# A trunk layer on one core: the mixer norm's strided sums replaced by a diagonal, and the softmax's division moved to GpSimd

## The chip, the cores and the metric

One core of a Trainium2 chip runs the whole layer. The metric is device microseconds (us) of one execution, the median of several runs. The engines are called by the names of the profile: PE (TensorE, with PEld for its weight loads), DVE (VectorE), ACT (ScalarE), POOL (GpSimd) and SP (the queue that issues the weight DMAs).

## The reference

The layer takes 512 tokens of 1024 features. It runs a half-step SwiGLU, then a mixer, a second half-step SwiGLU, a gated embedding and a last RMSNorm. The change lies in the mixer:

```
u = rmsnorm(h, g_mix)
z = u @ w_in                      # q, k, v (8 heads of 64), forget gate, SSM input
logits = q k^T / 8 + c_q - c_k    # c: running sum of log forget gates, causal mask
w = softmax(logits)               # rows in blocks of 128 queries
attn = w @ v
ssm  = s5_mixer(SSM input)        # runs beside the attention
h = h + concat(rmsnorm(attn), rmsnorm(ssm)) @ w_out
```

Everything is float32. Each matrix product is done as three products of split operands (a high part of type fp32r and the rest).

## The kernel before, in words

**Layout and order.** Activations lie with features on the partitions and the 512 tokens along the free axis, eight tiles `X[k]` of 128x512. The kernel's instructions are put out by hand in one order: `run` goes through a list of units; each has two steps, a step being some 12 matmuls on PE. Around each step, `run` takes one slot: it splits the weights of the next unit on ACT (`whi`) and DVE (`wlo`), runs evictions that have come due (`evicts`), advances the generators in `chains` by one `yield` before the step and by one after it, and runs what was put into `late` and `posts`. Each engine executes its own instructions strictly in that order. Weights come over SP's queue into five `wraw` tiles.

**The mixer's norm.** `Norm.chain` turns the accumulated squares `acc` (128 features x 512 tokens) into the reciprocal root mean square of each token. For each block of 128 tokens it multiplies `acc` as the stationary operand by a column of constants (line 316), which gives a sum for each token, tokens on the partitions. DVE adds EPS (line 322), POOL raises to the power -1/2 (line 323, `rc`), PE broadcasts `rc` over all partitions with four products by the identity (line 327), and ACT copies that to `r` (line 331, tile `rbc`). For the mixer's norm `n2` the chain is called with `strided=True`: four more sums are then taken over every fourth token, `acc[:, i::4]` (line 319), since the SSM input is computed with tokens j, j+4, j+8, ... on the partitions. Columns 4 to 7 of `rc` scale that input in `ssm_chain` (`ut`, line 714), columns 0 to 3 scale `v`. This chain runs while PE computes the forget gate's unit (lines 961 and 962, two steps of 8 matmuls).

**The attention.** It is a generator that advances with the slots from the second query/key unit on, beside the SSM's generator. Two heads (h2 = 0, 1) go together, in three stages: query blocks 0 and 1 (rows of 128 and 256 keys), block 2 (384) and block 3 (512). `SCORES` sets the slot n in which a stage's scores are multiplied (lines 1054, 1055, after the step). Then: at n+1, before the step, DVE adds the mask and takes the row's minimum (`exps`, line 1067; the sign is turned, so it is the maximum), and ACT gets the exponentials with their sums; at n+2, before the step, `divide` (lines 1080 and 1083): DVE takes the reciprocal of the sums and multiplies each block's row by it; at n+3, after the step, PE transposes the probabilities (`turn`, line 1091); at n+4 ACT and DVE split them (`pa`, `pb`, `pc`); `values_out` multiplies by `v` (lines 1136, 1137). PSUM is a ring of eight banks, `tmp` a ring of ten tiles of 128x512. POOL's own work in this stretch is the eight casts of `selr` into `qsel` (line 1034), two for each pair of heads, and the two DMA issues of `pr` (line 1226).

The two places in the code:

```
act(x, x, AF.Exp, scale=-1.0, bias=mn[h2][:, j:j + 1], accum_out=rs[h2][:, j:j + 1])
...
for hp, st in plan.get(n - 1, []):
    *state[hp, st], exp = exps(st, state[hp, st])
    late.insert(at_front, exp)
for hp, st in plan.get(n - 2, []):
    state[hp, st] = divide(st, *state[hp, st])
yield
...
chain_at(u_s[0], n2.chain(strided=True, wait=2))
```

Of the kernel before, what the change touches and what calls it, by code (L numbers as in the profile page):

```python
# [13 lines left out]
ADD, SUB, MUL = ALU.add, ALU.subtract, ALU.mult  # L14
# [28 lines left out]
def hybrid_trunk_kernel(ctx: ExitStack, tc: tile.TileContext, xT, pT, w13a, w2a, w13b, w2b, wqk, wv, ws, wf,  # L43
                        wglu, wout, wgate, wproj, cols, bf, ssm_s, ssm_bc, dskip, outT, dbg=None):
    nc = tc.nc
    V, S, G, T = nc.vector, nc.scalar, nc.gpsimd, nc.tensor
# [8 lines left out]
    def nm(base):  # L55
        n_name[0] += 1
        return f"{base}_{n_name[0]}"
# [7 lines left out]
    def tmp(shape=(128, 512), base="t"):  # L65
        return pool.tile(list(shape), F32, name=nm(base), tag="tmp", bufs=10)

    def small(shape, base="sm"):
        return pool.tile(shape, F32, name=nm(base), tag="small", bufs=12)

    def bank():
        return psum.tile([128, 512], F32, name=nm("ps"), tag="ps", bufs=8)
# [21 lines left out]
    ident = const.tile([128, 128], F32, name="ident")  # L94
# [160 lines left out]
    class Norm:  # L255
# [52 lines left out]
        def chain(self, strided=False, wait=0):  # L308
            for _ in range(2 * wait):
                yield  # L310
            yield
            one = ones[:, 0:1] if self.width == D else ones[:, 1:2]
            ps = bank()
            n = 8 if strided else 4
            for i in range(4):
                T.matmul(ps[:, i:i + 1], self.acc[:, i * 128:(i + 1) * 128], one, start=True, stop=True)  # L316
            if strided:
                for i in range(4):
                    T.matmul(ps[:, 4 + i:5 + i], self.acc[:, i::4], one, start=True, stop=True)
            yield  # L320
            ms, rc = small([128, 8], "ms"), small([128, 8], "rc")
            V.tensor_scalar(ms[:, 0:n], ps[:, 0:n], EPS, None, ADD)
            G.tensor_tensor(rc[:, 0:n], ms[:, 0:n], mhalf[:, 0:n], ALU.pow)
            yield
            ps = bank()
            for i in range(4):
                T.matmul(ps[:, i * 128:(i + 1) * 128], rc[:, i:i + 1].to_broadcast([128, 128]), ident,  # L327
                         start=True, stop=True)
            yield
            r = pool.tile([128, L], F32, name=nm("rbc"), tag="rbc", bufs=2)  # L330
            S.copy(r, ps)
            self.r, self.rc = r, rc
            yield


# [703 lines left out]
    def attention(qk, vs, nrm_a):  # L1039
# [38 lines left out]
        def divide(st, lg, rs):  # L1078
            for h2 in range(2):
                V.reciprocal(rs[h2][:, 0:len(BLOCKS[st])], rs[h2][:, 0:len(BLOCKS[st])])  # L1080
                for j, (i, c0) in enumerate(BLOCKS[st]):
                    x = lg[h2][:, c0:c0 + (i + 1) * 128]
                    V.tensor_scalar(x, x, rs[h2][:, j:j + 1], None, MUL)
            return lg

        def turn(st, lg):
# [75 lines left out]
        for n in range(VALUES[3] + 2):  # L1162

            at_front = len(late)
            for hp, st in plan.get(n - 4, []):
                if st == 0:
                    pt[hp] = probs()
                late.extend(split_probs(st, state.pop((hp, st)), pt[hp]))
            if po is not None:
                late.extend(gather(*po))  # L1170
                po = None
# [6 lines that stand above are left out]
            for hp, st in plan.get(n, []):  # L1178
                state[hp, st] = scores(hp, st)
            if n in VALUES:  # L1180
                hp = VALUES.index(n)
                po = hp, values_out(hp, pt.pop(hp))
            for hp, st in plan.get(n - 3, []):
                state[hp, st] = turn(st, state[hp, st])
            yield
# [391 lines left out]
```

## Time and profile before

| | |
|---|---|
| median of 3 runs | 1016.0 us (1014.75 to 1016.76) |
| profiled execution, its own time | 1014.84 us |
| its span | 1013.1 us |
| mean granted clock of TensorE | 0.995 |
| PE busy | 1000.1 us, 99% of the span |
| DVE busy | 663.0 us, 65% |
| ACT busy | 420.4 us, 41% |
| POOL busy | 44.6 us, 4% |

The profiled execution is 1.2 us faster than the median of the runs, and 1.7 us of its time lie outside the span. Busy time of PE counts a matmul to its modelled end; the spacing of two matmuls' starts tells more about its pace than their durations. The granted clock is a share of 2.4 GHz: 1.00 is 2.4 GHz and 0.50 is 1.2 GHz.

### The profile page before, as it was taken

The numbers are of one execution on the slowest core, as the hardware profiler recorded it, in microseconds if no ns is written. First come the engines' busy times: TensorE is split into PE (matmuls) and PEld (weight loads), VectorE is DVE, ScalarE is ACT, GpSimd is POOL, SyncE is SP. The second block draws the span as 40 slices with busy tenths as digits, with TensorE's granted clock in tenths as the row PEclk, the third lists the DMA queues.
The fourth block names the chain that finished last, engine by engine and source line by source line (L and its number), as shares of the span: only waits on it lengthen the run. The fifth ranks groups of instructions, "written<-read, shape, count | busy, mean of one in ns | idle before, by whom it ended". The sixth has DMA issues, their size and how long they took to land.

```text
span 1013.1 us, 13761 instructions
## 1 busy us (share of the span) xinstructions
PE 1000.1 (99%) x4988; PEld 840.8 (83%) x4988; DVE 663.0 (65%) x1321; ACT 420.4 (41%) x799; POOL 44.6 (4%) x52
## 2 busy tenths in 40 slices
PE   9999999999999999999999999999999999999996
PEld 7888888888878889888887888888888888888896
DVE  6678688767655564889998865444455446655465
ACT  6333233332343343468896443332332224434332
POOL 0430000001000001000101000000000000000000
PEclk9999999999999999999999999999999999999998
DMA  6423323233245332122112232333323335533002
GB/s 209 150 90 91 109 94 103 78 91 105 94 104 130 95 85 74 63 67 87 55 52 79 88 94 94 102 91 99 105 93 87 97 107 157 165 85 105 32 1 83
DMA packets 58244, 96.06 MB, mean 95 GB/s; under 512 B 10224, under 2 KB 17008, under 8 KB 58176
## 3 DMA queue, kind: packets, MB, share of 16 engines
q1 hardware_dynamic: 57920, 94.63, 30.9%
q8 instruction: 39, 0.64, 0.3%
q0 software_dynamic: 256, 0.56, 0.2%
q14 instruction: 29, 0.24, 0.1%
HBM read 91.89 MB, written 2.10 MB: 93 GB/s over the span
## 4 chain that ended last, share of the span: by engine, by line
PE 88%; DVE 7%; ACT 3%; issue 1%; DMA 0%; POOL 0%; SPq 0%; POOLq 0%; DVEq 0%; ACTq 0%
PE ps L236 28%; PE ps L238 28%; PE ps L237 28%; PE ps L1455 1%; DVE wlo L75 1%; DVE rot L75 1%; DVE lg L1067 1%; DVE qkhl L75 1%; ACT lg L81 1%; PE ps L327 1%; DVE rc L75 1%; PE ps L316 0%; PE ps L1091 0%; PE ps L640 0%; DVE U L738 0%
## 5 line engine op out<-in xcount | busy, mean ns | idle before, releaser
L236 PE MATMUL ps<-xhl,whi 128*128 128x512 f32 x816 | 320.3, 393 | 0.0
L238 PE MATMUL ps<-xhl,whi 128*128 128x512 f32 x816 | 317.8, 390 | 0.0
L237 PE MATMUL ps<-xhl,wlo 128*128 128x512 f32 x816 | 317.7, 389 | 0.0
L160 ACT CAST whi<-wraw 128x512 fp32r<-128x512 f32 x324 | 195.8, 607 | 240.2 <-PE ps L238 177.4
L75 DVE TENSOR_TENSOR wlo<-wraw,whi 128x512 fp32r<-128x512 f32 x324 | 215.5, 670 | 5.8 <-ACT whi L160 5.6
L238 PEld LDWEIGHTS ps<-xhl,whi 128*128 128x128 f32 x816 | 153.2, 188 | 32.4
L236 PEld LDWEIGHTS ps<-xhl,whi 128*128 128x128 f32 x816 | 153.2, 188 | 32.1 <-issue 1.0
L237 PEld LDWEIGHTS ps<-xhl,wlo 128*128 128x128 f32 x816 | 153.3, 188 | 31.1
L236 PE MATMUL ps<-h,whi 128*128 128x512 f32 x352 | 137.3, 390 | 0.0
L238 PE MATMUL ps<-h,whi 128*128 128x512 f32 x352 | 137.0, 389 | 0.0
L237 PE MATMUL ps<-h,wlo 128*128 128x512 f32 x352 | 137.0, 389 | 0.0
L78 DVE SCALAR_TENSOR_TENSOR x<-ps,x 128x512 f32<-128x512 f32 x48 | 33.2, 691 | 95.2 <-PE ps L238 95.1
L78 DVE SCALAR_TENSOR_TENSOR t<-ps,rbc 128x512 f32<-128x512 f32 x44 | 30.3, 690 | 76.5 <-PE ps L238 76.5
L238 PEld LDWEIGHTS ps<-h,whi 128*128 128x128 f32 x352 | 66.1, 188 | 13.8
L237 PEld LDWEIGHTS ps<-h,wlo 128*128 128x128 f32 x352 | 66.1, 188 | 13.7
L236 PEld LDWEIGHTS ps<-h,whi 128*128 128x128 f32 x352 | 66.1, 188 | 13.6
L75 DVE TENSOR_TENSOR t<-ps,rbc 128x512 f32<-128x512 f32 x44 | 30.4, 691 | 71.1 <-PE ps L238 65.0
L81 ACT ACTIVATE th<-t 128x512 f32<-128x512 f32 x44 | 27.8, 632 | 91.1 <-DVE t L75 91.1
L362 ACT CAST h<-t 128x512 fp32r<-128x512 f32 x44 | 27.4, 622 | 80.2 <-DVE t L75 80.2
L81 ACT ACTIVATE xhl<-x,colt 128x512 fp32r<-128x512 f32 x32 | 23.0, 725 | 47.8 <-DVE x L78 41.1
L236 PE MATMUL ps<-xhl,gw 128*128 128x256 f32 x128 | 36.5, 285 | 0.0
L238 PE MATMUL ps<-xhl,gw 128*128 128x256 f32 x128 | 36.2, 283 | 0.0
(256 smaller groups left out, 1134.5 us busy)
## 6 DMA issues: line engine op xcount, KB each, us to landing
wraw<-w13b SPq DMA_DIRECT2D x88, 256.0 KB, 2.9
wraw<-w13a SPq DMA_DIRECT2D x84, 256.0 KB, 2.8
wraw<-w2a SPq DMA_DIRECT2D x32, 256.0 KB, 2.7
wraw<-w2b SPq DMA_DIRECT2D x32, 256.0 KB, 2.7
wraw<-wqk SPq DMA_DIRECT2D x16, 256.0 KB, 2.8
wraw<-wout SPq DMA_DIRECT2D x16, 256.0 KB, 2.8
wraw<-wgate SPq DMA_DIRECT2D x16, 256.0 KB, 2.9
wraw<-w2a SPq DMA_DIRECT2D x16, 192.0 KB, 2.4
```

The costliest lines, as they stand in the source:

```text
L75: V.tensor_tensor(out, a, b, op)
L78: V.scalar_tensor_tensor(out, a, s, b, op0, op1)
L81: S.activation(out, in_, f, **kw)
L160: S.copy(hi[:, 0:n], w[:, 0:n])
L236: T.matmul(ps, lh, rh, start=start, stop=False)
L237: T.matmul(ps, ll, rh, start=False, stop=False)
L238: T.matmul(ps, lh, rl, start=False, stop=stop)
L327: T.matmul(ps[:, i * 128:(i + 1) * 128], rc[:, i:i + 1].to_broadcast([128, 128]), ident, start=True, stop=True)
L362: S.copy(hl[:, 0, :], box["t"])
L1067: V.tensor_tensor_reduce(lg[h2][:, c0:c0 + n], pss[h2][:, c0:c0 + n], maskp[:, 512 - n:512], 1.0, 3e38, ADD, ALU.min, mn[h2][:, j:j + 1])
L1455: T.matmul(box0[wi], fw[wi][2 if i == 1 else 1][:, k], n1.pair(k)[i == 2], start=k + i == 0, stop=k + i == KD + 1)
```

## The change

The norm's four strided sums go. In their place, after `r` (the broadcast reciprocal, the same in all partitions) is there, DVE takes from every fourth column of `r` the diagonal: it multiplies by the identity and sums along the row, so that partition p gets the value of token 4p + j. The multiplication of the probabilities goes from DVE to POOL; the reciprocal stays on DVE.

```
--- before.py
+++ after.py
@@ -311,12 +311,9 @@
             one = ones[:, 0:1] if self.width == D else ones[:, 1:2]
             ps = bank()
-            n = 8 if strided else 4
+            n = 4
             for i in range(4):
                 T.matmul(ps[:, i:i + 1], self.acc[:, i * 128:(i + 1) * 128], one, start=True, stop=True)
-            if strided:
-                for i in range(4):
-                    T.matmul(ps[:, 4 + i:5 + i], self.acc[:, i::4], one, start=True, stop=True)
             yield
@@ -330,6 +327,11 @@
             r = pool.tile([128, L], F32, name=nm("rbc"), tag="rbc", bufs=2)
             S.copy(r, ps)
             self.r, self.rc = r, rc
+            if strided:
+
+                dg = tmp((128, 4, 128), "dg")
+                for j in range(4):
+                    V.tensor_tensor_reduce(dg[:, j], r[:, j::4], ident, 1.0, 0.0, MUL, ADD, rc[:, 4 + j:5 + j])
             yield
@@ -1080,7 +1082,7 @@
                 for j, (i, c0) in enumerate(BLOCKS[st]):
                     x = lg[h2][:, c0:c0 + (i + 1) * 128]
-                    V.tensor_scalar(x, x, rs[h2][:, j:j + 1], None, MUL)
+                    G.tensor_scalar(x, x, rs[h2][:, j:j + 1], None, MUL)
             return lg
```

## Rows read from the trace of the kernel before

**Rows 1.** The page: busy time, share of the span and instructions of each engine.

```profile
PE 1000.1 (99%) x4988; PEld 840.8 (83%) x4988; DVE 663.0 (65%) x1321; ACT 420.4 (41%) x799; POOL 44.6 (4%) x52
```

**Rows 2.** Busy time by stretch: from:to, length, engines, PEclk, DMA share, GB/s.

```profile
386.00:387.00 1.00, 1.00 (x4) 0.52 (x3) 0.46 (x1) 0.00 (x0) 1.00 (x1) 0.50 0.02 4
...
546.40:548.00 1.60, 1.60 (x13) 1.46 (x12) 0.52 (x2) 0.22 (x1) 0.18 (x1) 1.00 0.47 145
```

**Rows 3.** Timeline around the mixer norm's sums: start, us, engine, instruction, [idle before].

```profile
380.39 0.39 PE L961 MATMUL ps<-xhl,wfh 128*64 128x512 f32 x1
...
382.23 0.95 PE L316 MATMUL ps<-ones,acc 128*128 128x1 f32 x8
...
383.04 2.00 PE L319 MATMUL ps<-ones,acc 128*128 128x1 f32 x8
...
384.90 0.42 PE L961 MATMUL ps<-xhl,wfh 128*64 128x512 f32 x1
...
385.33 2.04 POOL L323 TENSOR_TENSOR rc<-ms,mhalf 128x8 f32<-128x8 f32 x1 [80.19 <-DVE ms L322]
...
389.17 0.60 PE L236 MATMUL ps<-whi,xhl 128*128 128x512 f32 x1
```

**Rows 4.** Timeline of PE at the SSM output norm's broadcast.

```profile
550.17 1.05 PE L327 MATMUL ps<-ident,rc 128*128 128x128 f32 x8
550.98 0.48 PE L236 MATMUL ps<-xhl,whi 128*128 128x512 f32 x1
```

**Rows 5.** Timeline of ACT and DVE behind the mixer norm's chain.

```profile
389.45 0.59 ACT L331 COPY rbc<-ps 128x512 f32<-128x512 f32 x1 [10.98 <-PE ps L327]
...
391.19 0.68 DVE L75 TENSOR_TENSOR fz<-ps,fl 8x512 f32<-8x512 f32 x1 [4.73 <-ACT fl L968]
...
404.95 0.48 DVE L714 TENSOR_SCALAR ut<-ps,rc 128x256 f32<-128x256 f32 x1 [1.06 <-ACT ut L81]
```

**Rows 6.** Groups of DVE instructions from 460 to 545 us, by form: xcount | busy, mean ns.

```profile
L1067 DVE CUSTOM_DVE_ANT_0 lg<-ps,maskp 128x128 f32<-128x128 f32 x8 | 2.3, 282 | 0.0
```

**Rows 7.** Busy time from 460 to 545 us, all engines, then line 1083 alone.

```profile
460.00:545.00 85.00, 81.88 (x432) 69.16 (x431) 83.14 (x235) 75.74 (x195) 5.19 (x8) 1.00 0.20 63
...
460.00:545.00 85.00, 12.80 (x32) 1.00 0.20 63
```

**Rows 8.** Timeline of PE in the attention.

```profile
471.01 0.82 PE L1091 MATMUL ps<-ident,lg 128*128 128x128 f32 x6
...
474.44 0.22 PE L1054 MATMUL ps<-kcum,qsel 128*128 128x128 f32 x1
475.62 0.30 PE L1055 MATMUL ps<-qkhl,qkhl 128*128 128x128 f32 x1 [0.96 <-DVE qkhl L75]
...
534.14 0.88 PE L1091 MATMUL ps<-ident,lg 128*128 128x128 f32 x6 [1.52 <-ACT pp L81]
```

**Rows 9.** Who waited for whom, 460 to 545 us: us in total, times, longest.

```profile
ACT kcum L1015 <- DVE qk L78: 3.8, 3, 1.8
```

**Rows 10.** Groups of POOL instructions, whole span, by form: xcount | busy, mean ns.

```profile
L323 POOL TENSOR_TENSOR rc<-ms,mhalf 128x4 f32<-128x4 f32 x5 | 6.2, 1232 | 471.4 <-DVE ms L322 471.4
L1034 POOL CAST qsel<-selr 64x512 fp32r<-64x512 f32 x8 | 5.3, 662 | 111.4 <-PE ps L1054 111.0
...
L1353 POOL TENSOR_TENSOR o<-xg,r 128x256 f32<-128x256 f32 x2 | 1.4, 722 | 1.9 <-ACT r L1347 1.9
```

**Rows 11.** Timeline of POOL and DVE around the divisions.

```profile
467.84 1.42 POOL L1034 CAST qsel<-selr 64x512 fp32r<-64x512 f32 x2 [79.12 <-PE ps L1054]
...
468.07 0.72 DVE L1083 TENSOR_SCALAR lg<-lg,rs 128x128 f32<-128x128 f32 x2
468.72 0.15 DVE L1080 RECIPROCAL rs<-rs 128x2 f32<-128x2 f32 x1
...
485.16 0.82 DVE L1083 TENSOR_SCALAR lg<-lg,rs 128x128 f32<-128x128 f32 x2
...
523.24 0.55 DVE L1083 TENSOR_SCALAR lg<-lg,rs 128x128 f32<-128x128 f32 x2
```

More of the change, by code (lines that the diff above doesn't have):

```diff
@@ L313, in chain @@
             ps = bank()
-            n = 8 if strided else 4
+            n = 4
             for i in range(4):
                 T.matmul(ps[:, i:i + 1], self.acc[:, i * 128:(i + 1) * 128], one, start=True, stop=True)
-            if strided:
-                for i in range(4):
-                    T.matmul(ps[:, 4 + i:5 + i], self.acc[:, i::4], one, start=True, stop=True)
             yield
@@ L332, in chain @@
             self.r, self.rc = r, rc
+            if strided:
+                dg = tmp((128, 4, 128), "dg")
+                for j in range(4):
+                    V.tensor_tensor_reduce(dg[:, j], r[:, j::4], ident, 1.0, 0.0, MUL, ADD, rc[:, 4 + j:5 + j])
             yield
@@ L1082, in divide @@
                     x = lg[h2][:, c0:c0 + (i + 1) * 128]
-                    V.tensor_scalar(x, x, rs[h2][:, j:j + 1], None, MUL)
+                    G.tensor_scalar(x, x, rs[h2][:, j:j + 1], None, MUL)
             return lg
```

## The prediction

> **What bounds the kernel now.** I read the page first. PE is busy for 1000.1 of 1013.1 us [rows 1], so over the whole span only two things can save time: matmuls that go, or come faster, and places where PE waits. A change on DVE or POOL counts only through the second. Then I asked for the two stretches that the diff touches, as timelines and as busy time by stretch, since a share over the span says nothing of them.
>
> The first stretch is the mixer norm, 380 to 390 us. The reader is to see three things in rows 3 and 2. The four plain sums take from 382.23 to 383.04, 0.81 us, and the four strided sums from 383.04 to 384.90, 1.86 us: more than twice as long for the same count. After them PE's granted clock is 0.50, that is 1.2 GHz [rows 2]. So the forget gate's second step and the broadcast, which follow, run at half pace: from 384.90 to 389.17, 4.27 us [rows 3]. Last, POOL's power over eight columns lasts 2.04 us [rows 3], and PE needs it for the broadcast.
>
> The second stretch is the attention, 460 to 545 us. There DVE is the fullest engine: busy for 83.14 of 85.00 us, against 81.88 for PE and 75.74 for ACT; the divisions are 12.80 us of DVE's time in 32 instructions [rows 7]. PE waits here, which it hardly does elsewhere. I add up, from start to start, what each late instruction took beyond the same step at a place without a wait. There are six such places; the first is 474.44 to 475.62 us, where the score product waits for DVE's `qkhl`, and the last is the transposes that start at 534.14 us, 1.5 us idle behind ACT [rows 8]. Together they make 4.8 us; by the records alone PE is idle for 85.00 − 81.88 = 3.1 us [rows 7], but a wait also spreads two starts whose records touch. ACT, for its part, waits three times, 3.8 us in all, for DVE's `qk` [rows 9]: DVE's lateness is passed on to ACT, and ACT's to PE through the PSUM banks.
>
> **The change part by part.**
>
> *The strided sums go.* The forget gate's second step then starts at 383.04 instead of 384.90 us. Its eight matmuls took 382.23 − 380.39 = 1.84 us in the first step, at full clock [rows 3], so the broadcast is due at 384.88 us. Its input: the power began 385.33 − 384.90 = 0.43 us after the last sum had been followed by the next matmul [rows 3], so now at 383.47; over four columns it takes 1.23 us (mean of five) [rows 10] and ends at 384.70, just in time. The broadcast takes 550.98 − 550.17 = 0.81 us where the clock is full [rows 4], so the next unit's first matmul comes at 385.69 instead of 389.17 us: 3.5 us. This takes the clock to stay at 1.00. For it speaks that the same four sums without the strided ones, at the SSM output norm, are followed by 1.00 [rows 2], as at the kernel's other norms. Against it: only here do the sums lie between matmuls that load 64 columns instead of 128 [rows 3]. If the clock falls all the same, what is left is the removed time, 1.9 us. Ends: −1.9 and −3.5; I take −3.5, since the nearest rows are those of the other norms.
>
> *The diagonal.* Four reduces of 128x128 on DVE. The nearest row is the masked minimum of that size, 0.28 us [rows 6]; four are 1.1 us. Reading every fourth column may cost more; with twice the price it is 2.3 us. DVE has been idle for 4.73 us when its next instruction starts at 391.19 [rows 5]; the reduces can begin only when ACT has copied `r`, at 389.45 + 0.59 = 390.04 [rows 5], so the cheap price is hidden entirely and the dear one delays the forget gate's small chain by 1.1 us, whose result the attention wants some 70 us later. The first reader of the new columns, `ut`, comes at 404.95 [rows 5], 13 us on. If that cover were gone, the delay would hit the SSM's input by at most 2.3 us. The extra tile takes one of ten in `tmp`'s ring for about a microsecond. Cost: 0 (0 to 0.3).
>
> *The divisions on DVE go.* DVE is relieved of 12.80 us in 85 [rows 7]. What is late today because DVE is late: the score product at 475.62, three groups of transposes that wait for banks, and ACT's waits. ACT is next: 75.74 us of work in a stretch that would be 85.0 − 4.8 = 80.2 us long, 94%. So I expect the waits behind DVE to go and the last one, behind ACT at 534.14 us, to stay for the greater part: ACT loses its waits, but PE arrives earlier too. I keep 1.5 us of the 4.8.
>
> *The divisions on POOL.* The trace has no such instruction. They have one tensor input, 32 of them with 2 x 4 x (128 + 256 + 384 + 512) = 10,240 elements per partition. Nearest below: the cast, one input, 662 ns for 512 elements, 1.29 ns each; above: the two-input product, 722 ns for 256, 2.82 ns each [rows 10]. That is 13.2 to 28.9 us for all. I take 15, nearer to the cast, which also has one input. POOL does 5.19 us of other work in the 85 [rows 7], so it is not full in either case. Is it in time? The tightest place is the first stage: the second reciprocal (468.72 us, some 468.1 when no division stands ahead of it) to the transposes at 471.01 [rows 8, 11] leaves 2.9 us for 768 elements, that is 1.0 to 2.2 us of work. The other stages' transposes stand further behind. So no wait of PE: 0, and with all at the dear end and slowed, up to 1 us at the first stage. What stands behind the divisions in POOL's queue: the casts of `qsel` and the two DMA issues of `pr`. The casts at 467.84 would come after the first divisions and end at 471.8 us at the latest; they are read at 474.44 [rows 8, 11]. The DMA issues move back to the unit in which they are written, and still stand ahead of the projection units by several steps. SP's queue is untouched.
>
> *What POOL takes from DVE.* While POOL casts, two divisions on DVE took 0.72 and 0.82 us; with POOL idle, 0.55 [rows 11]. So DVE lost up to 0.27 of 0.82 us, 33%, where both read and write SBUF. On 15 us of POOL work, with half of DVE's instructions reading two SBUF tensors, I put the loss at 15 x 0.33 x 0.5 = 2.5 us of DVE's time (0 to 9.5 us, the latter from 28.9 x 0.33). DVE keeps a relief of about 10 us, enough for the above; I put another 0.3 us of PE's waits on it. The Trainium skill (SBUF — State Buffer, "Who interferes with whom") says more: a DVE instruction with two SBUF inputs and a GpSimd instruction that reads SBUF exclude each other for the whole instruction. The rows show a loss of a third under the casts, not a full stop; by the page's rule the relief would be eaten, which is the second rival.
>
> *Sum:* −3.5 + 0 − (4.8 − 1.5 − 0.3) = −6.5 us. On the profiled execution's own 1014.84 us this gives 1008.3; the median of the runs stands 1.2 us higher, so I forecast 1009.5 us.
>
> **The rivals.**
>
> *The clock falls anyway* (0.50 after the sums, between matmuls of 64 columns). Then −1.9 − 3.0: 1011.1 us. The other norms speak against it.
>
> *The relief is eaten.* Each microsecond of POOL is taken from DVE: 83.14 − 12.80 + 13.2 = 83.5 us, DVE is as full as before, PE's waits stay, and only the norm's 3.5 us are won: 1012.5 us. The 33% of rows 11 speaks against a full loss; that DVE's instructions with two SBUF inputs under a POOL that reads 128 partitions aren't in the trace speaks for it. With the first rival on top it is 1014.1 us, no change.
>
> *Slower: POOL blocks DVE at the dear price.* If POOL needs 28.9 us and all of that is DVE's loss, DVE has 83.14 − 12.80 + 28.9 = 99.2 us to do in 85, and PE follows: 1016.0 − 3.5 + 14.2 = 1026.7 us. It decides where DVE's loss is more than 12.80 + 3.5 = 16.3 us, that is over 56% of POOL's dear time. 33% lies below that.
>
> **How the numbers follow.** The forecast has 57%, the clock that falls 11%, the eaten relief 18%, both at once 6%, the slower case 8%. The likeliest case's own range is from −8.3 (3.5 and all 4.8 us) to −4.5: 1007.7 to 1011.5 us. The range of 8 in 10 takes in the first two rivals: 1007.4 to 1013.2 us. Measurement tells about 0.2%, 2 us, from no change: faster means below 1014.0, which holds for the forecast and for the first two rivals but for their upper ends: 83%. Within 0.2%: both at once and some of the eaten relief, 10%. Slower: 7%.
>
> **What the profile after would show.** Right: no line for strided sums, the granted clock at 1.00 throughout 382 to 390 us, and the distance from the plain sums to the next unit's first matmul 3.46 us instead of 6.94; four reduces on DVE just ahead of `fz`; DVE below 90% in the attention, POOL at about 20 us there; no wait for `qkhl`; a shorter wait or none of ACT for `qk`. Wrong: 0.50 behind the sums; two-input DVE instructions of 128x512 well above the 0.68 us of `fz` [rows 5] while POOL divides; transposes that wait for POOL's `lg`; or an ACT so full that PE's waits move behind it unshortened. The last is the weakest step: 1.5 us kept of 4.8 is a judgement between 0 and all.

## The result, and the profile after

The changed kernel takes 1009.4 us (median of 4 runs, 1009.11 to 1009.82) against 1015.6 us for the kernel before on the same chip (4 runs, 1014.75 to 1016.76): 0.9939 of its time, with a 95% interval of 0.9925 to 0.9953. On another chip it took 1010.1 against 1015.45 us, 0.9947 (0.9934 to 0.9961). The forecast was 1009.5 us.

The profiled execution took 1009.63 us, with a span of 1007.9 us. The page's busy times, beside [rows 1]:

```profile
PE 996.2 (99%) x4980; PEld 838.5 (83%) x4980; DVE 655.1 (65%) x1297; ACT 420.7 (42%) x799; POOL 83.8 (8%) x84
```

POOL has 39.2 us more to do, while DVE has lost only 7.9 us. That is the first surprise: the divisions were 12.80 us on DVE, and 13.2 to 28.9 us had been put down for POOL.

Next, busy time by stretch (from:to, length, PE, PEld, DVE, ACT, POOL, granted clock, DMA share, GB/s): the norm, the microsecond that was at 0.50 in [rows 2], and the attention from its first score product to the first matmul behind its last value product.

```profile
382.23:386.00 3.77, 3.77 (x24) 2.70 (x23) 0.77 (x2) 0.00 (x0) 2.01 (x2) 1.00 0.15 22
386.00:387.00 1.00, 1.00 (x8) 1.00 (x8) 0.00 (x0) 0.41 (x1) 0.63 (x2) 1.00 0.48 180
457.33:537.77 80.44, 79.09 (x425) 67.80 (x424) 72.66 (x201) 74.79 (x192) 44.55 (x40) 1.00 0.20 66
```

The clock stays at 1.00. In the attention DVE is busy for 72.66 of 80.44 us, 90%, and ACT, with 93%, is the fuller of the two.

The timeline of the norm (start, us, engine, instruction, idle before), beside [rows 3, 5]:

```profile
382.68 0.95 PE L316 MATMUL ps<-ones,acc 128*128 128x1 f32 x8
383.49 0.43 PE L963 MATMUL ps<-xhl,wfh 128*64 128x512 f32 x1
383.92 1.43 POOL L320 TENSOR_TENSOR rc<-ms,mhalf 128x4 f32<-128x4 f32 x1 [78.32 <-DVE ms L319]
385.40 0.97 PEld L324 LDWEIGHTS ps<-ident,rc 128*128 128x128 f32 x8 [0.34 <-POOL rc L320]
385.40 1.16 PE L324 MATMUL ps<-ident,rc 128*128 128x128 f32 x8
386.31 0.60 PE L236 MATMUL ps<-whi,xhl 128*128 128x512 f32 x1
387.21 0.39 DVE L334 CUSTOM_DVE_ANT_0 dg<-rbc,ident 128x128 f32<-128x128 f32 x1 [2.77 <-ACT rbc L328]
389.08 0.67 DVE L75 TENSOR_TENSOR fz<-ps,fl 8x512 f32<-8x512 f32 x1
```

From the first sum to the next unit it is 386.31 − 382.68 = 3.63 us, against 6.94. The four reduces, 0.37 to 0.39 us each, lie between 387.21 and `fz` at 389.08, and DVE had been idle for 2.77 us ahead of them.

The timeline of PE and POOL at the attention's first stages, beside [rows 8, 11]:

```profile
468.15 0.60 PE L1093 MATMUL ps<-ident,lg 128*128 128x128 f32 x4
469.85 0.44 PE L1093 MATMUL ps<-ident,lg 128*128 128x128 f32 x2 [1.10 <-POOL lg L1085]
...
472.88 0.22 PE L1056 MATMUL ps<-kcum,qsel 128*128 128x128 f32 x1
...
474.48 0.55 PE L1093 MATMUL ps<-ident,lg 128*128 128x128 f32 x3 [0.19 <-POOL lg L1085]
...
465.38 4.41 POOL L1085 TENSOR_SCALAR lg<-lg,rs 128x128 f32<-128x128 f32 x4 [78.70 <-issue]
469.86 2.12 POOL L1036 CAST qsel<-selr 64x512 fp32r<-64x512 f32 x2
471.97 6.06 POOL L1085 TENSOR_SCALAR lg<-lg,rs 128x384 f32<-128x384 f32 x4
```

Those two are the only waits of PE that the trace shows in the attention. The waits for `qkhl` and behind ACT at the last transposes [rows 8] are gone, and ACT's three waits for `qk` [rows 9] appear no more. In their place PE waits twice for POOL. The casts end at 469.86 + 2.12 = 471.98 us, 0.9 us before `qsel` is read.

POOL's groups over the whole span (count, busy us, mean ns, idle before), beside [rows 10]:

```profile
L1085 POOL TENSOR_SCALAR lg<-lg,rs 128x512 f32<-128x512 f32 x8 | 12.9, 1623 | 0.0
L1085 POOL TENSOR_SCALAR lg<-lg,rs 128x384 f32<-128x384 f32 x8 | 11.2, 1408 | 2.8 <-DVE rs L1082 2.8
L1085 POOL TENSOR_SCALAR lg<-lg,rs 128x256 f32<-128x256 f32 x8 | 7.9, 990 | 0.0
L1085 POOL TENSOR_SCALAR lg<-lg,rs 128x128 f32<-128x128 f32 x8 | 6.1, 760 | 95.1 <-issue 78.7 <-DVE rs L1082 16.4
```

The divisions take 12.9 + 11.2 + 7.9 + 6.1 = 38.1 us, three times what they took on DVE.

**Where the time came from.** In the two profiled executions the norm gives 6.94 − 3.63 = 3.31 us and the attention 83.50 − 80.44 = 3.06 us. Between them (71.02 us) nothing changes. The rest goes the other way: 0.45 us at the start, 0.71 us behind the attention. Together they make the 5.2 us by which the spans differ. The kernels below show no pattern in either: the part behind the attention is 469.4 us in before and between 469.3 and 470.5 in the others, with 469.8 in the one whose norm and attention are those of before (power in two). The trace names no cause.

### The profile page after: what moved, and what is told of

It is laid out like the page before. It is cut to its first block, busy times and chain, and to the rows that moved or that the text cites. A ratio compares the mean times of both kernels' runs of the same rounds, so it can differ in the third digit from the quotient of the medians.

```text
span 1007.9 us, 13796 instructions
## 1 busy us (share of the span) xinstructions
PE 996.2 (99%) x4980; PEld 838.5 (83%) x4980; DVE 655.1 (65%) x1297; ACT 420.7 (42%) x799; POOL 83.8 (8%) x84
## 4 chain that ended last, share of the span: by engine, by line
PE 91%; DVE 5%; ACT 1%; issue 1%; DMA 1%; POOL 0%; SPq 0%; POOLq 0%; ACTq 0%; DVEq 0%
PE ps L236 29%; PE ps L238 29%; PE ps L237 28%; PE ps L1457 1%; PE ps L1093 1%; DVE rot L75 1%; DVE wlo L75 1%; DVE rc L75 1%; PE ps L324 1%; PE ps L1139 1%; PE ps L316 0%; PE ps L1138 0%; DMA x<-xT 0%; DVE qkhl L75 0%; PE ps L642 0%
## 5 line engine op out<-in xcount | busy, mean ns | idle before, releaser
L320 POOL TENSOR_TENSOR rc<-ms,mhalf 128x4 f32<-128x4 f32 x6 | 8.0, 1338 | 519.6 <-DVE ms L319 519.6
L1085 POOL TENSOR_SCALAR lg<-lg,rs 128x128 f32<-128x128 f32 (+3 forms) x32 | 37.8, 1195 | 97.9 <-issue 78.7
```

The costliest lines, as they stand in the source:

```text
L1085: G.tensor_scalar(x, x, rs[h2][:, j:j + 1], None, MUL)
```

## The experiments

In the first table "norm" is the time from the first plain sum to the next unit's first matmul, "attention" that of the last row of the windows above. Times with an interval, and that of before, are medians of several runs; the others are single executions. Norm and attention are always those of one profiled execution. The kernels ran on several chips; each interval compares with the kernel before on the same chip.

| kernel | norm | attention | time, us | beside before |
|---|---|---|---|---|
| before | 6.94 | 83.50 | 1015.6 | |
| after | 3.63 | 80.44 | 1009.4 | 0.9939 (0.9925 to 0.9953) |
| after, second chip | 3.63 | 80.50 | 1010.1 | 0.9947 (0.9934 to 0.9961) |
| diagonal alone | 3.63 | 83.52 | 1012.4 | 0.9965 (0.9952 to 0.9978) |
| POOL alone | 6.89 | 80.58 | 1012.7 | 0.9971 (0.9961 to 0.9982) |
| sums contiguous | 5.14 | 83.56 | 1013.7 | |
| strided sums later | 5.48 | 83.58 | 1014.0 | |
| power in two | 6.93 | 83.53 | 1015.7 | |
| no division | 3.63 | 79.16 | 1009.5 | |
| POOL's work beside | 3.63 | 87.38 | 1016.0 | |
| price at the start | 3.63 | 80.54 | 1010.2 | |
| first stages on DVE | 3.64 | 80.16 | 1009.5 | 0.9942 (0.9929 to 0.9954) |
| one head on DVE | 3.64 | 79.35 | 1009.0 | 0.9938 (0.9924 to 0.9952) |

### The two halves

The diagonal alone: the changed kernel with the division back on DVE.

```
-                    G.tensor_scalar(x, x, rs[h2][:, j:j + 1], None, MUL)
+                    V.tensor_scalar(x, x, rs[h2][:, j:j + 1], None, MUL)
```

> Only the norm's part of the change; the division stays on VectorE. Theory (removed sums plus the clock that no longer falls): from the plain sums to the next unit's first matmul 3.6 us instead of 6.94, granted clock 1.00 there, and the attention (first score product to the first matmul behind the last value product) as long as before, 83.5 us: 3.3 us in all, about 0.3% faster. Rival (the two parts help each other: PE arrives earlier at a stage that VectorE fills, so the gain is lost there): the attention grows by up to 3.3 us and the kernel is no faster.

POOL alone: the kernel before with the opposite edit of that line.

> Only the division's part of the change; the strided sums stay. Theory (VectorE's relief): the norm takes 6.94 us as before, with the clock at 0.50 behind it, and the attention is 80.4 us long instead of 83.5: 3.1 us, about 0.3% faster. Rival (the attention's gain came from the norm's earlier end): the attention stays at 83.5 us, no faster.

Measured: 1012.4 and 1012.7 us beside 1015.6 us. The gains, 3.2 and 2.95 us, add up to the 6.2 us of the whole change, so the runs show no effect of one half on the other. In the diagonal alone the attention is that of before, as its windows row and its waits (who for whom, us, times, longest) show:

```profile
457.15:540.67 83.52, 80.38 (x425) 67.91 (x424) 81.69 (x232) 74.42 (x192) 5.19 (x8) 1.00 0.20 64
```

```profile
ACT kcum L1017 <- DVE qk L78: 3.8, 3, 1.8
...
PE ps L1093 <- ACT pp L81: 1.5, 1, 1.5
```

DVE fills 98% of the stretch. In POOL alone the norm is that of before (6.89 us), the strided sums and the late broadcast included.

### Which sums bring the clock down in the norm

Sums contiguous: the kernel before, with as many sums, but the second four read `acc` in contiguous blocks again. Columns 4 to 7 then scale the SSM input with other tokens' values.

```
-                    T.matmul(ps[:, 4 + i:5 + i], self.acc[:, i::4], one, start=True, stop=True)
+                    T.matmul(ps[:, 4 + i:5 + i], self.acc[:, i * 128:(i + 1) * 128], one, start=True, stop=True)
```

> The kernel before, with the four strided sums taken over contiguous blocks of 128 tokens instead (so columns 4 to 7 scale the SSM's input with other tokens' values): the same count of sums, without the stride. Theory (the stride makes a sum dear, 0.23 against 0.10 us each of eight passes): the eight sums take 1.6 us instead of 2.67, and the clock, after a shorter thin stretch, stays at 1.00: 7 - 1.1 - 1.6 = 4.4 us from the first sum to the next unit. Rival (the count of thin sums makes the clock fall): 1.6 us of sums, then 0.50 behind them, 5.8 us in all.

Strided sums later: the kernel before again, without the diagonal, but the strided sums get a bank of their own and come behind the broadcast; EPS and the power for their columns follow.

```
+            if strided:
+                ps2 = bank()
+                for i in range(4):
+                    T.matmul(ps2[:, i:i + 1], self.acc[:, i::4], one, start=True, stop=True)
...
+                V.tensor_scalar(ms[:, 4:8], ps2[:, 0:4], EPS, None, ADD)
+                G.tensor_tensor(rc[:, 4:8], ms[:, 4:8], mhalf[:, 0:4], ALU.pow)
```

> The kernel before, with the strided sums kept but issued one step later, behind the broadcast, with a power of their own; the result is the same. Theory (the long thin stretch, not the strided reads as such, makes the clock fall): with eight full matmuls and the broadcast between the two groups of sums the clock stays at 1.00 and the whole takes 0.8 + 1.84 + 0.9 + 1.9 = 5.4 us, 1.5 us less than before. Rival (strided sums let it fall wherever they stand): 0.50 for some 4 us behind them, hidden nowhere: 5.4 us and then about 1.6 us more in the next unit.

Both norms became shorter, 5.14 and 5.48 us. The timelines, first of the contiguous sums with the window of the microsecond behind, then the same of the later ones:

```profile
383.07 1.03 PE L319 MATMUL ps<-ones,acc 128*128 128x1 f32 x8
383.96 0.43 PE L961 MATMUL ps<-xhl,wfh 128*64 128x512 f32 x1
...
386.49 1.16 PE L327 MATMUL ps<-ident,rc 128*128 128x128 f32 x8 [0.48 <-POOL rc L323]
...
385.00:386.00 1.00, 1.00 (x5) 0.33 (x3) 0.52 (x1) 0.00 (x0) 1.00 (x1) 1.00 0.08 18
```

```profile
385.50 1.16 PE L324 MATMUL ps<-ident,rc 128*128 128x128 f32 x8
386.49 1.92 PE L329 MATMUL ps<-ones,acc 128*128 128x1 f32 x8
388.27 0.61 PE L236 MATMUL ps<-whi,xhl 128*128 128x512 f32 x1
...
389.00:390.00 1.00, 1.00 (x6) 1.00 (x6) 0.97 (x3) 0.00 (x0) 1.00 (x1) 1.00 0.00 0
```

Four contiguous sums take 383.96 − 383.07 = 0.89 us, four strided ones 388.27 − 386.49 = 1.78 us: the stride doubles them wherever they stand. The clock stays at 1.00 behind eight contiguous sums, so their number is not what makes it fall, and behind four strided ones at the later place. It was 0.50 behind 2.67 us of sums in one go (382.23 to 384.90) [rows 2, 3]. Each of these readings of the clock is from one execution. Whether four strided sums alone, at the place of the plain ones, would leave it at 1.00 was not tried. The contiguous sums were expected to do better than they did; the broadcast waited 0.48 us for the power over eight columns [rows 3]. So I tried that power by itself.

Power in two: the kernel before, with the power taken over four columns at a time.

```
-            G.tensor_tensor(rc[:, 0:n], ms[:, 0:n], mhalf[:, 0:n], ALU.pow)
+            for i in range(0, n, 4):
+                G.tensor_tensor(rc[:, i:i + 4], ms[:, i:i + 4], mhalf[:, i:i + 4], ALU.pow)
```

> The kernel before with its strided sums, but the power over eight columns taken as two over four, so the broadcast needs only the first, which ends about 0.6 us sooner. Theory (the matmuls at 1.2 GHz and the long power run side by side, and either alone makes the broadcast late): the clock falls as before and the broadcast still starts no sooner than eight matmuls at half pace allow: 6.6 to 6.9 us from the first sum to the next unit. Rival (the long power is what kept the broadcast): 6.3 us or less.

The norm stays at 6.93 us, and the kernel at 1015.7 us beside 1015.4. Its timeline:

```profile
385.80 2.40 POOL L324 TENSOR_TENSOR rc<-ms,mhalf 128x4 f32<-128x4 f32 x2 [80.19 <-DVE ms L322]
...
388.27 0.63 PE L963 MATMUL ps<-xhl,wfh 128*64 128x512 f32 x1
388.70 1.17 PE L328 MATMUL ps<-ident,rc 128*128 128x128 f32 x8
```

PE goes from the last half-pace matmul to the broadcast without a gap, 388.70 − 388.27 = 0.43 us. Pace and power run side by side: with the clock at 0.50 the power is hidden, with the clock at 1.00 the power over eight columns is the next limit, the 0.48 us of the contiguous sums. The diagonal removes both, since it also brings the power down to four columns.

### What the divisions cost, and whom

No division: the probabilities stay undivided, and POOL has nothing to do for them.

```
                 for j, (i, c0) in enumerate(BLOCKS[st]):
-                    x = lg[h2][:, c0:c0 + (i + 1) * 128]
-                    G.tensor_scalar(x, x, rs[h2][:, j:j + 1], None, MUL)
+                    pass
```

> The changed kernel without any multiplication by the reciprocal (the probabilities stay unnormalised), on neither engine. Theory (all of PE's waits in the attention hang on VectorE's load, and what is left after the change on GpSimd's price): no wait at all, 83.5 - 4.8 = 78.7 us. Rival (ACT, 94% full, sets a limit of its own): PE's last transposes still wait for ACT, 79.5 us or more.

The windows row of its attention:

```profile
458.65:537.81 79.16, 78.99 (x425) 67.91 (x424) 70.47 (x201) 74.27 (x192) 5.64 (x8) 1.00 0.20 67
```

This is the floor: 79.16 us. The rival, that ACT keeps the attention at 79.5 us or more, falls; ACT is 94% full and yet PE waits nowhere behind it but for 0.17 us. And it gives POOL's price for DVE: the same 201 instructions of DVE keep it busy for 70.47 us here and 72.66 us in the changed kernel, 2.2 us more under 37.8 us of divisions (POOL's busy time; their durations add up to 38.1). The kernel's time, 1009.5 us, does not show the shorter attention, since its norm starts at 383.92 us, 1.24 us later than in the changed kernel; the trace names no cause.

Price at the start: the changed kernel, with POOL's multiplication in four sizes at its start, ahead of most of DVE's work, and two sizes with a constant in place of the column.

```
+    for q in (128, 256, 384, 512):
+        G.tensor_scalar(pt_[:, 0:q], maskp[:, 0:q], half[:, 0:1], None, MUL)
+    for q in (128, 512):
+        G.tensor_scalar(pt_[:, 0:q], maskp[:, 0:q], 0.5, None, MUL)
```

> The changed kernel with six multiplications more at the very start, on GpSimd alone, ahead of any work of VectorE: 128, 256, 384 and 512 columns by a column of scalars, then 128 and 512 columns by a constant; their result is read by nobody. Question: is GpSimd's division dear by itself (1.62 us for 512 columns, 0.76 for 128 in the changed kernel), or because VectorE uses the shared ports? Theory (its own price for the most part): 1.4 us for 512 columns and 0.55 for 128. Rival (contention): the price of the cast, 0.66 us for 512. The attention is as in the changed kernel, 80.4 us.

POOL's groups of that kernel:

```profile
L123 POOL TENSOR_SCALAR price<-maskp,half 128x512 f32<-128x512 f32 x1 | 1.7, 1669 | 0.1
L125 POOL TENSOR_SCALAR price<-maskp 128x512 f32<-128x512 f32 x1 | 1.6, 1577 | 0.1
...
L123 POOL TENSOR_SCALAR price<-maskp,half 128x128 f32<-128x128 f32 x1 | 0.6, 612 | 0.0
```

The two sizes between took 0.92 and 1.24 us. A constant in place of the column saves next to nothing. So most of the price is the instruction's own. The rest shows in the changed kernel's attention, instruction by instruction: 25 of the 32 divisions take 0.60 to 0.61, 0.92 to 0.93, 1.23 to 1.24 and 1.55 to 1.56 us, by size, which makes 8 x (0.60 + 0.92 + 1.24 + 1.56) = 34.6 us for all. The other seven are 0.19 to 0.94 us longer, and each of the seven began while DVE was in an instruction with two inputs from SBUF, such as `ghl` or `wlo`; of the 25 one did, in the last 0.11 us of such an instruction. Two of them stand in the very first group. The timeline of POOL and DVE in the changed kernel, one instruction a line, for that group and for a later division:

```profile
465.18 0.67 DVE L78 SCALAR_TENSOR_TENSOR ghl<-gel,ghl 128x512 fp32r<-128x512 f32 x1
465.38 1.47 POOL L1085 TENSOR_SCALAR lg<-lg,rs 128x128 f32<-128x128 f32 x1 [78.70 <-issue]
465.77 0.68 DVE L75 TENSOR_TENSOR wlo<-wraw,whi 128x512 fp32r<-128x512 f32 x1
466.85 0.92 POOL L1085 TENSOR_SCALAR lg<-lg,rs 128x256 f32<-128x256 f32 x1
467.75 0.60 POOL L1085 TENSOR_SCALAR lg<-lg,rs 128x128 f32<-128x128 f32 x1
468.32 0.68 DVE L78 SCALAR_TENSOR_TENSOR ghl<-gel,ghl 128x512 fp32r<-128x512 f32 x1
468.33 1.47 POOL L1085 TENSOR_SCALAR lg<-lg,rs 128x256 f32<-128x256 f32 x1
...
491.59 1.55 POOL L1085 TENSOR_SCALAR lg<-lg,rs 128x512 f32<-128x512 f32 x1
491.73 1.08 DVE L75 TENSOR_TENSOR wlo<-wraw,whi 128x512 fp32r<-128x512 f32 x1
```

Beside `ghl` and `wlo` the first 128x128 took 1.47 us, the second 0.60; beside `ghl` the second 128x256 took 1.47 us, the first 0.92. It goes the other way too: `wlo` at 491.73, under a division, took 1.08 us, where the 19 `wlo` in the attention of the diagonal alone take 0.67 to 0.69.

POOL's work beside: the divisions are on DVE, as in the diagonal alone, and POOL does as many multiplications of the same sizes into a tile that nobody reads.

```
+            junk = tmp(base="junk")
...
-                    G.tensor_scalar(x, x, rs[h2][:, j:j + 1], None, MUL)
+                    V.tensor_scalar(x, x, rs[h2][:, j:j + 1], None, MUL)
+                    G.tensor_scalar(junk[:, 0:(i + 1) * 128], maskp[:, 0:(i + 1) * 128], rs[h2][:, j:j + 1], None, MUL)
```

> The norm's part of the change; the division stays on VectorE, and GpSimd does the same 32 multiplications beside it on a constant tile, at the same points, into a tile that nobody reads: the cost of GpSimd's work on VectorE by itself. Theory (a loss of about a third of the overlap where VectorE reads two SBUF tensors): VectorE's two-input instructions of 128x512 average 0.75 us instead of 0.68 and the attention grows from 83.5 to about 86 us. Rival (full exclusion): VectorE loses most of GpSimd's 38 us, the attention exceeds 100 us. Second rival (no cost): 83.5 us.

The attention takes 87.38 us, 3.9 us more than the 83.52 of the diagonal alone, for 39.8 us of POOL's work. Its windows row, then a DVE group of this kernel, then two of the diagonal alone:

```profile
457.21:544.59 87.38, 81.78 (x425) 69.19 (x424) 85.87 (x231) 74.72 (x192) 44.66 (x40) 0.98 0.18 61
```

```profile
L1086 DVE TENSOR_SCALAR lg<-lg,rs 128x384 f32<-128x384 f32 x8 | 4.7, 591 | 0.3
```

```profile
L1085 DVE TENSOR_SCALAR lg<-lg,rs 128x512 f32<-128x512 f32 x8 | 3.9, 486 | 0.3
...
L1085 DVE TENSOR_SCALAR lg<-lg,rs 128x384 f32<-128x384 f32 x8 | 3.4, 421 | 0.3
```

DVE is busy for 85.87 us instead of 81.69, 4.2 us more. Its multiplications of 128x384 became 40% longer on the mean (591 against 421 ns); the stretch as a whole grew by a tenth of POOL's time. Nothing waits for the dead tile in the trace, so it is not the tile ring that holds the others up. But the 3.9 us are not POOL's alone: behind PE's waits between 471 and 495 us, 3.4 us in all, the granted clock was 0.50 for some 3 us from 496 us on, and PE's busy time is 1.4 us longer than in the diagonal alone. So neither view at the ends is right: POOL is not free for DVE, and is far from stopping it.

### Where POOL is late

The first group of four divisions took 4.41 us. The same four take 2.98 to 3.18 us in the three later groups, and their undisturbed times add up to 2 x (0.60 + 0.92) = 3.04 us. With these the first group would have ended at 465.38 + 3.04 = 468.42 us; the two transposes that waited were due at 469.85 − 1.10 = 468.75 us. So by this estimate POOL's own price would have made nobody wait here, and the 1.10 us come from the two divisions that DVE's instructions lengthened. The price kernel, where `qkhl` came beside the fourth division as well, bears it out (timelines of POOL and PE):

```profile
465.49 4.93 POOL L1090 TENSOR_SCALAR lg<-lg,rs 128x128 f32<-128x128 f32 x4 [78.77 <-issue]
...
470.47 0.44 PE L1098 MATMUL ps<-ident,lg 128*128 128x128 f32 x2 [1.61 <-POOL lg L1090]
```

The group is 0.52 us longer there and PE's wait 0.51 us. Nor is it the first use of the operation that costs, since this kernel had used it at its start. No run took DVE's instructions away from this place. The next two kernels take work from POOL instead.

First stages on DVE: of the first pair of heads, stages 0 and 1 are divided by DVE, the rest by POOL. One head on DVE: only the second head of the very first stage is.

```
+            eng = V if hp == 0 and st < 2 else G
...
-                    G.tensor_scalar(x, x, rs[h2][:, j:j + 1], None, MUL)
+                    eng.tensor_scalar(x, x, rs[h2][:, j:j + 1], None, MUL)
```

In one head on DVE the first of these lines, inside the loop over the heads, is instead:

```
+                eng = V if hp + st == 0 and h2 else G
```

> The changed kernel, but the first two stages of the first pair of heads are divided on VectorE, the other ten on GpSimd. Theory (what is left of PE's waits is GpSimd's lateness at these two stages, 1.1 and 0.2 us of idle time): no wait of the transposes for the division, the attention about 79.0 us instead of 80.4, 1.3 us faster than the changed kernel, 0.75% faster than the one before. Rival (VectorE is then late again with the query/key split, as in the kernel before): the wait for that product, about 1 us, comes back and the time is that of the changed kernel.

> The changed kernel, but of the very first stage the second head's two blocks are divided on VectorE; the other 30 divisions stay on GpSimd. Theory (at this stage alone GpSimd is late, and half its work fits into its 2.9 us, while VectorE gets only 0.65 us more and the query/key split had 1.3 us to spare): no wait for the division, at most a small one for the split, the attention 79.5 us instead of 80.4, about 0.9 us faster than the changed kernel in the trace. Rival (any division on VectorE at this place brings the wait for the split back, as with two whole stages there): 80.2 us or more.

With the first stages on DVE, PE's waits for POOL go, but the one for `qkhl` is back, 0.97 us: 80.16 us. DVE has no room there for both stages. With one head on DVE, POOL's first group has two divisions and takes 2.50 us (timeline of POOL, then of PE):

```profile
465.43 2.50 POOL L1086 TENSOR_SCALAR lg<-lg,rs 128x128 f32<-128x128 f32 x2 [78.66 <-issue]
...
472.02 0.33 PE L1057 MATMUL ps<-qkhl,qkhl 128*128 128x128 f32 x1 [0.16 <-ACT qkhl L1028]
```

That 0.16 us is PE's only wait left in the attention, which takes 79.35 us, 0.2 above the floor. The time, 1009.0 us (1008.1 to 1009.8), can't be told from the changed kernel's by its runs; the trace alone shows the 1.1 us.

The changed kernel again, on the second chip, where first stages on DVE ran too (one head on DVE ran on a third):

> The changed kernel itself, for comparison on the same chip: 0.6% faster than the one before, the attention 80.4 us.

## Why the prediction was right

The forecast of 1009.5 us was met by 1009.4. That closeness is in part luck: the gain was put at 6.5 us from 1016.0 and came to 6.2 from 1015.6. Of the terms some held, and errors in the others cancelled.

**The norm, −3.5: held, −3.31.** The strided sums' 1.86 us went and the clock stayed at 1.00; the first rival (clock falls between matmuls of 64 columns) is refuted. What lacks, 0.17 us, is at the broadcast: its weight load waited 0.34 us for the power, which took 1.43 us instead of the mean of 1.23; it started 0.07 us later than reckoned and took 0.91 us, not 0.81. The step "just in time" was just not. The prediction priced the loss beyond 1.86 us by the clock alone; the contiguous sums show that the power over eight columns was a second limit behind it.

**The diagonal, 0: held.** Four reduces of 0.37 to 0.39 us, somewhat above the 0.28 us of the nearest row; they follow 2.77 us of DVE's idle time, and from the norm to the attention it is 71.02 us in both kernels.

**The waits behind DVE, 4.8: nearly.** The floor without division shows 83.50 − 79.16 = 4.34 us.

**What stays, 1.5 behind ACT: wrong in place.** PE's wait of 1.52 us behind ACT vanished whole, though ACT is as busy as in the diagonal alone (74.79 against 74.42 us); it had only handed on DVE's lateness. What stays is 80.44 − 79.16 = 1.28 us, and PE spends it waiting for POOL: with one head on DVE 1.09 of them go.

**POOL's divisions, 15 us of 13.2 to 28.9: the step that failed.** They take 38.1 us, 34.6 of them undisturbed, beyond the dear end either way. The nearest rows were a cast and a two-input product; neither bounds an operation with a column of scalars, 3.0 ns an element at 512, undisturbed (1.56 us). The slack at the first stage was right: from the end of the reciprocals, 465.04 + 0.22, to the transposes at 468.15 it is 2.9 us. But the four divisions take 4.41 us there, not 1.0 to 2.2. The prediction asked what POOL takes from DVE and not what DVE takes from POOL, which is 1.37 of the 4.41 us and by the estimate above the whole wait. "Up to 1 us at the first stage", meant for the dear end and slowed divisions, is what came: 1.10 us. It is also one of the signs that the prediction had set down for being wrong, transposes that wait for POOL's `lg`. Two of the signs for being right failed: POOL is busy for 44.55 us in the attention and not about 20, and DVE for 90%, not below. The casts behind them, too, had 0.9 us left where 2.6 us had been reckoned.

**What POOL takes from DVE, 2.5 us: 2.2 us, by luck,** as 6% of 38 us and not 17% of 15 us. The share of a third, from the casts, was too high for these instructions, and the time too low. The second rival (relief eaten) and the slower one both needed DVE to lose most of POOL's time; had DVE lost a third of POOL's 38 us, that is 12.5 us, next to nothing of the 12.8 us would have been left. By the rule of the Trainium skill that the prediction named (SBUF — State Buffer, "Who interferes with whom") one of two such instructions holds the other off for its whole length. The trace agrees in that divisions of POOL that began beside such an instruction of DVE became up to 0.94 us longer. It doesn't bear out a full stop of DVE: `wlo` at 491.73 became 0.40 us longer, under a division of which 1.41 us were still to come and which kept its undisturbed 1.55 us. Of the 19 `wlo` in the changed kernel's attention 15 kept their 0.67 to 0.69 us, five of these with a division under way beside them.

So the sum was right because the residue wrongly put behind ACT (1.5 us) has the size of the one that POOL's late divisions make (1.3 us). That is luck: no step of the prediction ties the two.

## What to carry to other kernels

Work taken from a full engine pays as far as the waits that it caused, here 4.3 us for 12.8 us of relief, and on the slower engine only its tightest deadline counts: 38 us of POOL cost 1.3 us, 1.1 of them at the one stage with 2.9 us of slack for 4.4 us of work. Price an operation by a row of the same form; where there is none, widen the bound beyond the neighbours, and check the tightest deadline at the dear end. Where two engines slow each other, price both directions, at that deadline first: there the mean of all 32 instructions said little. When something slow is removed from a chain, look for what ran beside it, since that sets the time next.

## What the runs showed of the hardware

- A multiplication by a column of scalars on POOL takes 0.60 us for 128x128 and 1.56 us for 128x512 (float32) where nothing disturbs it, over three times the 0.49 us of 128x512 on DVE in the attention of the diagonal alone. A constant costs as much (1.58 us).
- A POOL division that began while DVE was in an instruction with two SBUF inputs became 0.19 to 0.94 us longer (seven of 32 in the changed kernel); four of the 19 `wlo` there became 0.04 to 0.40 us longer.
- Sums over a strided stationary operand take twice as long: 1.78 to 1.86 us for four against 0.81 to 0.89.
- The granted clock stayed at 1.00 behind 0.8 and 1.7 us of one-column products in one go, and behind 1.78 us of strided ones at the later place; it fell to 0.50 behind 2.67 us of them.
- The casts of `qsel` went from 662 to 854 ns on the mean of eight; the pair right behind the first divisions took 2.12 us, where 1.42 us had been the time of a pair before [rows 11]. In the changed kernel's attention five of the six took 0.96 to 1.10 us, and each of these began beside `qkhl` or `wlo`; the sixth, which did not, took 0.61 us.
